# Squares of the out projection and twenty weight sums from VectorE to GpSimd, in a hybrid encoder layer

## The chip, the cores and the metric

The kernel runs on one core of a Trainium2 chip. The metric is device time in microseconds (us), the median of several runs. The core has five engines with instruction queues of their own: TensorE (PE, its weight loads listed as PEld), VectorE (DVE), ScalarE (ACT), GpSimd (POOL) and SyncE (SP, which here only issues DMAs). Each engine works through its queue in order, and semaphores make it wait for the others.

## The reference

One layer of an encoder, for 1024 tokens of width 1024, all in float32:

```
hn   = rmsnorm(x, norm_mix)
proj = hn @ w_in                      # split into two groups of heads
o_a  = window_gqa_sink(...)           # window of 128 to both sides, sink logit
o_b  = neighbourhood_attention(...)   # 2-D window with a learned bias
mix  = concat(rmsnorm(o_a, norm_a), rmsnorm(o_b, norm_b))
h    = x + mix @ w_out                # 1024 x 1024
hn   = rmsnorm(h, norm_ffn)
g    = hn @ w_gate; u = hn @ w_up     # 1024 x 2816 each
g    = conv3(g, conv_w) + conv_b      # along the tokens, per feature
h    = h + (silu(g) * u) @ w_down     # 2816 x 1024
out  = rmsnorm(h, norm_final)         # rmsnorm(x, g) = x * rsqrt(mean(x*x) + 1e-6) * g
```

The change touches the stretch from `mix @ w_out` over the sums of squares of `rmsnorm(h, norm_ffn)` to the first columns of `hn @ w_gate` and `hn @ w_up`.

## The kernel before

**Layout.** Activations stand transposed: 128 features on the partitions, tokens along the free axis. The 1024 features are eight tiles, numbered by d or k, and the 1024 tokens two halves (h) of 512. A "half tile" is 128 x 512. `at(k, h)` is half h of tile k of the residual stream h1. Products keep float32 accuracy by splitting each operand into a high and a low float16 part. A high part is made by ScalarE (a scaled copy), the low part by VectorE (the operand minus the high part: L1151 and L1068 for weights, L1096 for `w_out`, L1184 for activations). Three matmuls then stand for one: high by high, high by low, low by high.

**Out projection** (the loop before L1300). For each half h and each of the eight output tiles d, which I write (h, d), `product16` (L176) issues twelve matmuls (four tiles with three each) into one of three PSUM banks; the other four input tiles went into h1 earlier. `settle_out` (L1196) follows:

- L1199, VectorE: h1 = bank * scale + h1, with priority 300 in the scheduler.
- L1200: h1 goes to DRAM by a DMA of ScalarE's queue; it is read again only in the last stage.
- L1203, ScalarE: the square of the half tile.
- L1205, VectorE: for d = 1 to 3, the square plus the running total.

So the first four squares of a half are one addend, and d = 4 to 7 are four more. `sum_up` (L1210) gives each addend to PE as four matmuls of a single column against a tile of 1/1024 (L1216), accumulated in a narrow bank of 128 x 4: one number for each token. `inverse_root` (L1219) adds 1e-6 (L1221, VectorE) and raises to the power -1/2 (L1222, GpSimd). `widen` (L259) then spreads the four columns over all partitions with four PE transposes (L263). `normed` (L1225; L1227, VectorE) multiplies h1 by this and by the gain, for tiles K1 (0 to 3) or K2 (4 to 7). `operands` splits the result (ScalarE, L1184). An older helper, `inverse_power` (L217), does the same from one full total: four transposes (L221), a reduce over VectorE (L223), scaling and 1e-6 (L224) and the power on GpSimd (L225); the two attention groups use it earlier in the kernel.

For half 0 `inverse_root` stands at (1, 1), `widen`, `normed` of K1 and their operands at (1, 2), `normed` of K2 at (1, 4).

**FFN by seven products.** The input tiles K1 and K2, the gate and up columns, and the two token halves make a 2 x 2 block product, computed with seven block products in place of eight. With g1, g2 the K1 and K2 rows of the gate weights and u1, u2 those of the up weights, the weights' operands are "11" = g1, "12" = g2, s1 = u1 + u2, s2 = s1 - g1, s4 = g2 - s2, s3 = g1 - u1, "22" = u2. The sums are made in one tile `ws` of each unit (`head_weights`, L1233; L1237 for s1, `sub`, L1229, for the others) and then split. On the other side stand the normed halves and their differences t1 to t4 (`sub`, L1229, in place in h1). One output tile of gate and up together is a unit; product p1 uses "11", p2 "12", p5 s1 and t1, p6 s2 and t2, p3 s4, p7 s3 and t3, p4 "22" and t4. Each is twelve matmuls (`group`, L1174 to L1178).

The first four units go through the products side by side (L1463 to L1521): p1 and p2 of units 0 and 1, p1 of 2 and 3, p2 of 2 and 3, then p5, p6, p3, p7, p4 of all four. Half 1's norm is needed from p5 on. Its sum and `inverse_root` stand after p2 of unit 0, `widen` after p2 of unit 1. The weights' sums of these units are made early: s1 and s2 during the out projection, s4 at (1, 4) to (1, 7), s3 and "22" in the loops of p3 and p7.

**What sets the order.** PE's instructions keep the order of the program. The other engines' order comes from the scheduler, which takes what is ready, moved ahead by `high_priority(offset=...)`; `behind(name)` holds an instruction back until the marked one stands in the order. After the change the lines below L1205 carry smaller numbers; the names and the arithmetic stay.

Of the kernel before, what the change touches and what calls it, by code (L numbers as in the profile page):

```python
# [13 lines left out]
F32 = mybir.dt.float32  # L14
# [8 lines left out]
KT = D // 128  # L23
# [40 lines left out]
def hybrid_layer(tc, xT, w_in, w_out, w_gate, w_up, w_down, small, sink, rpb, consts, rope, out):  # L64
    nc = tc.nc
    with ExitStack() as ctx:
# [25 lines left out]
        def bank(name, tag):  # L92
            return psum.tile([128, HALF], F32, name=name, tag=tag)
# [123 lines left out]
        def inverse_power(sq, dim, tag):  # L217

            ps = bank("st", tag)
            for c in range(4):  # L220
                nc.tensor.transpose(ps[:, c * 128:(c + 1) * 128], sq[:, c * 128:(c + 1) * 128], ident)  # L221
            v = cpool.tile([128, 4], F32, name="v4", tag="v4", bufs=4)
            nc.vector.tensor_reduce(v, ps[:, :].rearrange("p (c w) -> p c w", w=128), axis=mybir.AxisListType.X, op=ALU.add)  # L223
            nc.vector.tensor_scalar(v, v, 1.0 / dim, EPS, op0=ALU.mult, op1=ALU.add)  # L224
            nc.gpsimd.tensor_tensor(v, v, minus_half, op=ALU.pow)  # L225
            return v
# [965 lines left out]
        B = {}  # L1192
        late, total, addends, narrow, ADDED = [], [None, None], [], [None, None], (4, 4)
        at = lambda k, h: h1[k][:, tsl(h)]

        def settle_out():  # L1196
# [5 lines left out]
            with tc.high_priority(offset=300):  # L1202
                nc.scalar.activation(s2, at(d, h), AF.Square)  # L1203
                if 0 < d < ADDED[h]:
                    nc.vector.tensor_tensor(s2, s2, total[h], op=ALU.add)  # L1205
            total[h] = s2
            if d >= ADDED[h] - 1:
                addends.append((h, d, s2))

        def sum_up(until=2 * KT):  # L1210
            while addends and KT * addends[0][0] + addends[0][1] <= until:
                h, d, s2 = addends.pop(0)
                if d == ADDED[h] - 1:
                    narrow[h] = bank("ss", "pt")
                for c in range(4):
                    nc.tensor.matmul(narrow[h][:, c:c + 1], s2[:, c * 128:(c + 1) * 128], ones[:, 0:1], start=c == 0 and d == ADDED[h] - 1,  # L1216
                                     stop=d == KT - 1, skip_group_check=True)

        def inverse_root(h):  # L1219
            v = cpool.tile([128, 4], F32, name="v4", tag="v4", bufs=4)  # L1220
            nc.vector.tensor_scalar(v, narrow[h][:, 0:4], EPS, None, op0=ALU.add)  # L1221
            nc.gpsimd.tensor_tensor(v, v, minus_half, op=ALU.pow)  # L1222
            return v

# [4 lines left out]
        sub = lambda o, x, y: nc.vector.tensor_tensor(o, x, y, op=ALU.subtract)  # L1229

        wsum = [fpool.tile([128, 4, 128], F32, name="ws", tag="tt", bufs=8) for _ in range(HEAD)]

        def head_weights(i, name):  # L1233
            f, t = FO[i], wsum[i]
            g, u = head_raw[f]
            if name == "s1":
                nc.vector.tensor_tensor(t, u[:, 0:4], u[:, 4:8], op=ALU.add)  # L1237
            elif name == "s2":
                sub(t, t, g[:, 0:4])
            elif name == "s4":  # L1240
                sub(t, g[:, 4:8], t)
            elif name == "s3":
                sub(t, g[:, 0:4], u[:, 0:4])
            else:
                t = u[:, 4:8]
# [8 lines left out]

        S1_AT, S2_AT, S4_AT, SETTLE_AT, PURE_AT = [(0,3),(0,3),(0,4),(0,5)], [(1,0),(1,1),(1,2),(1,3)], [(1,4),(1,5),(1,6),(1,7)], {(0,1):0,(0,3):2}, {(0,2):(0,1),(0,4):(2,3)}
        for d in range(WO_EARLY, KT):
# [4 lines left out]
        for h in range(2):  # L1261
            for d in range(KT):
                if h == 0 and len(wo) < KT:
                    wo.append(load_wo(len(wo), fpool))
                ps = bank("pj", ("o", "s", "pj")[(h * KT + d) % 3])
                for _ in product16(ps, wo[d], mg[4:8], h):
                    pass
                late.append((d, h, ps))
                sum_up(KT * h + d - 2)
                if h == 1 and d == 1:  # L1270
                    with tc.high_priority(offset=300):
                        v = inverse_root(0)
                settle_out()
# [4 lines left out]
                for when, name in ((S1_AT, "s1"), (S2_AT, "s2"), (S4_AT, "s4")):  # L1278
                    for i, x in enumerate(when):
                        if x == (h, d):  # L1280
                            head_weights(i, name)
                if h == 1 and d == 2:
                    wide = widen(v, "pt")
                    normed(0, wide, K1)
                    B[1, 1] = operands([at(k, 0) for k in K1], "mix", "mix")
                if h == 1 and d == 4:
                    normed(0, wide, K2)
                    B[2, 1] = operands([at(k, 0) for k in K2], "mix", "mix")
# [175 lines left out]
        units[0].p1()  # L1464
        units[1].p1()
        units[0].p2()
        with tc.high_priority(offset=300):
            sum_up()
            v = inverse_root(1)
        units[1].p2()  # L1470
# [417 lines left out]
```

## Time and profile before

| | before |
|---|---|
| runs, us | 1036.99, 1037.27, 1037.58 |
| median, us | 1037.27 |
| span of the profiled execution, us | 1035.9 |
| PE matmuls, busy us | 1011.7 (98%) |
| VectorE, busy us | 880.0 (85%) |
| ScalarE, busy us | 679.3 (66%) |
| GpSimd, busy us | 214.1 (21%) |
| DMA | 191.28 MB |

The span runs from the first to the last instruction of one profiled execution; for that execution no other time is recorded, so the 1.4 us between it and the median stand for what lies around the span. Busy times count the work of each engine without its waits. In a row of groups, `out<-in` names the tiles, then come the shapes and types, the count, the busy time with the mean in nanoseconds of one, and the idle time ahead with what ended it. A row of the timeline is the start in us, the length, the engine and the instruction, and in brackets a wait and its releaser; the length of a row of several instructions (x4) runs from the start of the first to the end of the last.

### The profile page before, as it was taken

Reading aid. Unit: us, or ns where it says so; the run is one execution under the profiler, and the core shown is the slowest. Engines: PE = TensorE matmul, PEld = TensorE weight load, DVE = VectorE, ACT = ScalarE, POOL = GpSimd, SP = SyncE. Lnnn points to the kernel's source line nnn. Section 1 sums busy time; section 2 is a strip of 40 time slices with the busy share of each in tenths; the row PEclk is TensorE's granted clock in tenths of the full one; section 3 lists DMA queues with packets and bytes.
Section 4 is the critical chain, followed back from the end, with each engine's and each line's share of the span. In section 5 each row is a group of like instructions: output and inputs, shape, how many; then the busy total and the mean of one; then the engine's idle time right before and its main releaser. Section 6 shows DMA issues by size and latency. Waiting matters only on the chain.

```text
span 1035.9 us, 15696 instructions
## 1 busy us (share of the span) xinstructions
PE 1011.7 (98%) x5102; PEld 577.3 (56%) x5102; DVE 880.0 (85%) x1748; ACT 679.3 (66%) x1243; POOL 214.1 (21%) x341
## 2 busy tenths in 40 slices
PE   9998999999999999999999999999999999999996
PEld 7776777777775545544444444444444444444446
DVE  6699998766898699899898988888888879899875
ACT  8567787767687587645777777754535656655551
POOL 2235455676866301000000000000000000000002
PEclk9999999999999999999999999999999999999998
DMA  9447473676689775300687867733232778878744
GB/s 347 155 98 149 109 139 83 151 168 140 134 180 224 213 276 193 121 1 21 222 266 261 276 241 250 251 111 133 82 112 102 240 252 297 301 250 264 255 153 163
DMA packets 144275, 191.28 MB, mean 185 GB/s; under 512 B 77376, under 2 KB 88640, under 8 KB 144192
## 3 DMA queue, kind: packets, MB, share of 16 engines
q1 hardware_dynamic: 133536, 164.51, 54.7%
q10 hardware_dynamic: 10656, 25.76, 6.4%
q8 instruction: 40, 0.66, 0.2%
q14 instruction: 43, 0.35, 0.1%
HBM read 132.81 MB, written 28.57 MB: 156 GB/s over the span
## 4 chain that ended last, share of the span: by engine, by line
PE 71%; DVE 6%; ACT 1%; DMA 1%; issue 1%; POOL 0%; ACTq 0%; DVEq 0%; SPq 0%; POOLq 0%
PE dn L1177 6%; PE dn L1178 6%; PE dn L1176 6%; PE pj L180 6%; PE z L1176 5%; PE z L1177 5%; PE z L1178 5%; PE y L1176 4%; PE y L1177 4%; PE y L1178 4%; PE x L1176 4%; PE x L1177 4%; PE x L1178 3%; PE pj L172 2%; PE pj L174 2%; PE pj L173 2%
## 5 line engine op out<-in xcount | busy, mean ns | idle before, releaser
L1178 PEld LDWEIGHTS <-wlo 128*128 128x128 f16 x898 | 87.9, 98 | 101.3 <-DVE wlo L1151 0.2
L1176 PEld LDWEIGHTS <-whi 128*128 128x128 f16 x898 | 88.1, 98 | 100.3
L1177 PEld LDWEIGHTS <-whi 128*128 128x128 f16 x898 | 87.9, 98 | 100.3 <-issue 0.2
L1178 PE MATMUL dn<-xd,wlo 128*128 128x512 f16 (+1 forms) x330 | 120.4, 365 | 0.0
L1177 PE MATMUL dn<-xd,whi 128*128 128x512 f16 (+1 forms) x330 | 120.4, 365 | 0.0
L1176 PE MATMUL dn<-xd,whi 128*128 128x512 f16 (+1 forms) x330 | 120.4, 365 | 0.0
L172 PE MATMUL pj<-xgh,whi 128*128 128x512 f32 x248 | 106.8, 431 | 0.8 <-ACT whi L156 0.8
L1177 PE MATMUL z<-hg,whi 128*128 128x512 f16 x264 | 100.1, 379 | 0.0
L1178 PE MATMUL z<-hg,wlo 128*128 128x512 f16 x264 | 100.1, 379 | 0.0
L1176 PE MATMUL z<-hg,whi 128*128 128x512 f16 x264 | 100.1, 379 | 0.0
L466 ACT ACTIVATE p<-p,nm 128x385 f32<-128x385 f32 (+3 forms) x128 | 74.8, 585 | 38.0 <-DVE nm L462 33.3
L174 PE MATMUL pj<-xgh,wlo 128*128 128x512 f32 x248 | 97.9, 395 | 1.4 <-POOL wlo L157 1.4
L173 PE MATMUL pj<-xgl,whi 128*128 128x512 f32 x248 | 97.5, 393 | 0.0
L1150 ACT ACTIVATE whi<-ws,m 128x512 f16<-128x512 f32 (+1 forms) x96 | 65.9, 709 | 35.6 <-DVE ws L1317 19.5
L1151 DVE SCALAR_TENSOR_TENSOR wlo<-ws,m,whi 128x512 f16<-128x512 f32 (+1 forms) x96 | 70.2, 741 | 17.8 <-ACT whi L1150 17.6
L1031 POOL TENSOR_TENSOR back<-back,cst 128x4 f32<-128x4 f32 (+1 forms) x7 | 2.8, 396 | 356.7 <-DVE back L1030 356.7
L1165 ACT ACTIVATE scan<-scan 128x1024 f32<-128x1024 f32 (+1 forms) x60 | 61.1, 1019 | 17.0 <-DMA scan<-in_w_down_dram 12.3
L1150 ACT ACTIVATE whi<-raw,m 128x512 f16<-128x512 f32 (+1 forms) x78 | 51.4, 700 | 17.9 <-DMA raw<-in_w_down_dram 12.7
L1151 DVE SCALAR_TENSOR_TENSOR wlo<-raw,m,whi 128x512 f16<-128x512 f32 (+1 forms) x78 | 55.4, 732 | 7.5 <-ACT whi L1150 6.9
L1176 PE MATMUL y<-hg,whi 128*128 128x512 f16 x160 | 60.6, 379 | 0.0
L1177 PE MATMUL y<-hg,whi 128*128 128x512 f16 x160 | 60.6, 379 | 0.0
L1178 PE MATMUL y<-hg,wlo 128*128 128x512 f16 x160 | 60.6, 379 | 0.0
(291 smaller groups left out, 2465.5 us busy)
## 6 DMA issues: line engine op xcount, KB each, us to landing
xd<-x SPq DMA_DIRECT2D x77, 256.0 KB, 5.4
raw<-in_w_down_dram SPq DMA_DIRECT2D x64, 256.0 KB, 3.8
x<-c ACTq DMA_DIRECT2D x22, 512.0 KB, 3.5
scan<-in_w_gate_dram SPq DMA_DIRECT2D x18, 512.0 KB, 4.7
scan<-in_w_up_dram SPq DMA_DIRECT2D x18, 512.0 KB, 4.3
raw<-in_w_gate_dram SPq DMA_DIRECT2D x18, 512.0 KB, 3.8
raw<-in_w_up_dram SPq DMA_DIRECT2D x18, 512.0 KB, 4.4
raw<-in_w_in_dram SPq DMA_DIRECT2D x32, 256.0 KB, 3.1
```

The source lines that it names most:

```text
L172: nc.tensor.matmul(ps, w[0], x[0][:, tsl(h)], start=first, stop=False)
L173: nc.tensor.matmul(ps, w[0], x[1][:, tsl(h)], start=False, stop=False)
L174: nc.tensor.matmul(ps, w[1], x[0][:, tsl(h)], start=False, stop=last)
L180: nc.tensor.matmul(ps, a, b, start=i == 0 and b is x[h][0] and a is w[0], stop=i == len(ws) - 1 and a is w[1])
L466: nc.scalar.activation(p[:, 0:e], p[:, 0:e], AF.Exp, bias=nm, scale=-1.0, accum_out=sm)
L1031: nc.gpsimd.tensor_tensor(back, back, unit_back.to_broadcast([128, n]), op=ALU.mult)
L1150: mark["whi"] = nc.scalar.activation(hi, src, AF.Copy, scale=by)
L1151: nc.vector.scalar_tensor_tensor(lo, src, by, hi, op0=ALU.mult, op1=ALU.subtract)
L1165: nc.scalar.activation(t, t, AF.Square, accum_out=dst)
L1176: nc.tensor.matmul(ps, w[0], x[0], start=first and i == 0, stop=False, skip_group_check=True)
L1177: nc.tensor.matmul(ps, w[0], x[1], start=False, stop=False, skip_group_check=True)
L1178: nc.tensor.matmul(ps, w[1], x[0], start=False, stop=last and i == len(ws) - 1, skip_group_check=True)
```

## The change

1. **Sums of squares.** `sum_up`, `inverse_root` and the narrow bank go. All eight squares of a half are added up into one total: d = 1 to 6 on GpSimd, d = 7 on VectorE. The total goes through `inverse_power` (four transposes, reduce, scaling, power): for half 0 behind the first three matmuls of (1, 3), for half 1 after p1 of unit 1 and before p2 of unit 0.
2. **Half 0's norm.** `widen` and `normed` of K1 move from (1, 2) to (1, 4), with priority 150; `normed` of K2 from (1, 4) to (1, 5).
3. **Twenty sums on GpSimd.** s1, s2, s4 and s3 of the first four units, and the four differences for t4. s2 is held behind half 0's sum of d = 6, the s4, s3 and the differences behind the last power (mark "power" in L225).
4. **s4 of the first units** moves, sum and split, from (1, 4) to (1, 7) into the loop of p2 of units 2 and 3.

The diff, cut to its core:

```diff
-            nc.gpsimd.tensor_tensor(v, v, minus_half, op=ALU.pow)
+            mark["power"] = nc.gpsimd.tensor_tensor(v, v, minus_half, op=ALU.pow)
...
                 nc.scalar.activation(s2, at(d, h), AF.Square)
-                if 0 < d < ADDED[h]:
-                    nc.vector.tensor_tensor(s2, s2, total[h], op=ALU.add)
+                if d:
+                    mark["sum", d, h] = (nc.vector if d == KT - 1 else nc.gpsimd).tensor_tensor(s2, s2, total[h], op=ALU.add)
             total[h] = s2
-            if d >= ADDED[h] - 1:
-                addends.append((h, d, s2))
...
+        def slow(o, x, y, after):
+            with behind(after):
+                nc.gpsimd.tensor_tensor(o, x, y, op=ALU.subtract)
...
             if name == "s1":
-                nc.vector.tensor_tensor(t, u[:, 0:4], u[:, 4:8], op=ALU.add)
+                nc.gpsimd.tensor_tensor(t, u[:, 0:4], u[:, 4:8], op=ALU.add)
             elif name == "s2":
-                sub(t, t, g[:, 0:4])
+                slow(t, t, g[:, 0:4], ("sum", KT - 2, 0))
             elif name == "s4":
-                sub(t, g[:, 4:8], t)
+                slow(t, g[:, 4:8], t, "power")
             elif name == "s3":
-                sub(t, g[:, 0:4], u[:, 0:4])
+                slow(t, g[:, 0:4], u[:, 0:4], "power")
...
-                for _ in product16(ps, wo[d], mg[4:8], h):
-                    pass
+                for i, _ in enumerate(product16(ps, wo[d], mg[4:8], h)):
+                    if (h, d, i) == (1, 3, 0):
+                        with tc.high_priority(offset=300):
+                            v = inverse_power(total[0], D, "pt")
                 late.append((d, h, ps))
-                sum_up(KT * h + d - 2)
-                if h == 1 and d == 1:
-                    with tc.high_priority(offset=300):
-                        v = inverse_root(0)
...
-                if h == 1 and d == 2:
+                if h == 1 and d == 4:
                     wide = widen(v, "pt")
-                    normed(0, wide, K1)
-                    B[1, 1] = operands([at(k, 0) for k in K1], "mix", "mix")
-                if h == 1 and d == 4:
+                    with tc.high_priority(offset=150):
+                        normed(0, wide, K1)
+                        B[1, 1] = operands([at(k, 0) for k in K1], "mix", "mix")
+                if h == 1 and d == 5:
                     normed(0, wide, K2)
...
         units[1].p1()
+        with tc.high_priority(offset=300):
+            v = inverse_power(total[1], D, "pt")
         units[0].p2()
-        with tc.high_priority(offset=300):
-            sum_up()
-            v = inverse_root(1)
         units[1].p2()
...
-        for u in units[2:]:
+        for i, u in enumerate(units[2:]):
             u.p2()
+            for k in (2 * i, 2 * i + 1):
+                head_weights(k, "s4")
...
         for k in K1:
             sub(at(k, 0), at(k, 1), at(k, 0))
-            sub(at(k, 1), at(k + 4, 0), at(k, 1))
+        for k in K1:
+            slow(at(k, 1), at(k + 4, 0), at(k, 1), "power")
```

How this stands in the queues, in two places. GpSimd, from the end of half 0's out projection to half 1's power. Before, these rows follow each other (`back` and `taps` are the convolution's taps, `v4` the narrow result of a half):

```order
L1031 TENSOR_TENSOR back_5079<-back_5079,cst_89 128x2
L1034 TENSOR_SCALAR taps_5082<-par_79,back_5079 128x3
L1034 TENSOR_SCALAR taps_5084<-par_79,back_5079 128x3
L1222 TENSOR_TENSOR v4_5236<-v4_5236,minus_half_87 128x4
L1222 TENSOR_TENSOR v4_5483<-v4_5483,minus_half_87 128x4
```

After the change the stretch from half 0's sum of d = 6 to the power of half 0 reads as follows (`s2` are squares and their totals, `ws` the tile of a unit's weight sums, `rw` its raw weights; L1205 adds squares, L1216 is `slow`, L225 the power):

```order
L1205 TENSOR_TENSOR s2_5163<-s2_5163,s2_5142 128x512
L1216 TENSOR_TENSOR ws_4954<-ws_4954,rw_4745 128x512
L1216 TENSOR_TENSOR ws_4955<-ws_4955,rw_4747 128x512
L1216 TENSOR_TENSOR ws_4956<-ws_4956,rw_4749 128x512
L1216 TENSOR_TENSOR ws_4957<-ws_4957,rw_4751 128x512
L1205 TENSOR_TENSOR s2_5221<-s2_5221,s2_5199 128x512
L1205 TENSOR_TENSOR s2_5244<-s2_5244,s2_5221 128x512
L225 TENSOR_TENSOR v4_5261<-v4_5261,minus_half_87 128x4
```

Between the taps and the power there was nothing; now the four s2 and two sums of half 1 stand ahead of half 0's power.

VectorE, around half 1's norm. Before (L1221 is the addition of 1e-6, L1151 a low part of s4, L1317 and L1330 sums for the unit behind the first four, L1227 `normed`, L1229 `sub`):

```order
L1221 TENSOR_SCALAR v4_5483<-ss_5363 128x4
L1151 SCALAR_TENSOR_TENSOR wlo_5374<-ws_4955,m_5006,whi_5373 128x512
L1317 TENSOR_TENSOR ws_6006<-raw_5973 128x512
L1151 SCALAR_TENSOR_TENSOR wlo_5400<-ws_4956,m_5074,whi_5399 128x512
L1151 SCALAR_TENSOR_TENSOR wlo_5426<-ws_4957,m_5074,whi_5425 128x512
L1330 TENSOR_TENSOR ws_6046<-raw_5971,raw_5973 128x512
L1227 SCALAR_TENSOR_TENSOR h1_4134<-h1_4134,cst_89,sw_5500 128x512
```

After (L223 and L224 are the reduce and its scaling; L1303 and L1316 are the lines that were L1317 and L1330, L1210 the one that was L1227, `normed`):

```order
L1303 TENSOR_TENSOR ws_5984<-raw_5951 128x512
L223 TENSOR_REDUCE v4_5426<-st_5421 128x4
L1316 TENSOR_TENSOR ws_6024<-raw_5949,raw_5951 128x512
L224 TENSOR_SCALAR v4_5426<-v4_5426 128x4
L1151 SCALAR_TENSOR_TENSOR wlo_5527<-ws_4954,m_5006,whi_5526 128x512
L1151 SCALAR_TENSOR_TENSOR wlo_5532<-ws_4955,m_5006,whi_5531 128x512
L1151 SCALAR_TENSOR_TENSOR wlo_5551<-ws_4956,m_5074,whi_5550 128x512
L1151 SCALAR_TENSOR_TENSOR wlo_5556<-ws_4957,m_5074,whi_5555 128x512
L1210 SCALAR_TENSOR_TENSOR h1_4134<-h1_4134,cst_89,sw_5458 128x512
```

All four s4 splits now stand between the reduce and the first norm, and each takes its `ws` from GpSimd, which makes it after the power.

More of the change, by code (lines that the diff above doesn't have):

```diff
@@ L1192, in hybrid_layer @@
         B = {}
-        late, total, addends, narrow, ADDED = [], [None, None], [], [None, None], (4, 4)
+        late, total = [], [None, None]
         at = lambda k, h: h1[k][:, tsl(h)]
@@ L1203, in settle_out @@
                 nc.scalar.activation(s2, at(d, h), AF.Square)
-                if 0 < d < ADDED[h]:
-                    nc.vector.tensor_tensor(s2, s2, total[h], op=ALU.add)
+                if d:
+                    mark["sum", d, h] = (nc.vector if d == KT - 1 else nc.gpsimd).tensor_tensor(s2, s2, total[h], op=ALU.add)
             total[h] = s2
-            if d >= ADDED[h] - 1:
-                addends.append((h, d, s2))
[L1210 to L1223, printed above, removed]
         def normed(h, wide, ds):
@@ L1253, in hybrid_layer @@
         s1_places = []
-        S1_AT, S2_AT, S4_AT, SETTLE_AT, PURE_AT = [(0,3),(0,3),(0,4),(0,5)], [(1,0),(1,1),(1,2),(1,3)], [(1,4),(1,5),(1,6),(1,7)], {(0,1):0,(0,3):2}, {(0,2):(0,1),(0,4):(2,3)}
+        S1_AT, S2_AT, S4_AT, SETTLE_AT, PURE_AT = [(0,3),(0,3),(0,4),(0,5)], [(1,0),(1,1),(1,2),(1,3)], [None] * HEAD, {(0,1):0,(0,3):2}, {(0,2):(0,1),(0,4):(2,3)}
         for d in range(WO_EARLY, KT):
```

## The prediction

> **What bounds the kernel now.** The page first: TensorE (PE) is busy 98% of the span.
>
> ```profile
> span 1035.9 us, 15696 instructions
> PE 1011.7 (98%) x5102; PEld 577.3 (56%) x5102; DVE 880.0 (85%) x1748; ACT 679.3 (66%) x1243; POOL 214.1 (21%) x341
> ```
>
> Then the table of 10 us stretches over the place of the change (the out projection runs from 369 to 419, the first four FFN units from 419 to 494): busy time of PE, weight loads, VectorE (DVE), ScalarE, GpSimd (POOL), then clock and DMA.
>
> ```profile
> core 0: us, PE busy (x) PEld busy (x) DVE busy (x) ACT busy (x) POOL busy (x), PEclk, DMA share, GB/s
> 385.00:395.00 10.00, 10.00 (x61) 6.11 (x59) 10.00 (x17) 8.58 (x15) 1.68 (x3) 1.00 0.64 211
> 395.00:405.00 10.00, 10.00 (x59) 5.87 (x57) 8.72 (x15) 5.91 (x10) 1.39 (x1) 1.00 0.35 124
> 475.00:485.00 10.00, 10.00 (x48) 4.51 (x46) 10.00 (x12) 4.73 (x5) 0.00 (x0) 1.00 0.01 2
> ```
>
> PE never waits here, VectorE is full without making it wait, and GpSimd is nearly idle. So only two things count: PE work taken out, and new waits of PE. VectorE time saved is worth nothing by itself.
>
> **The change part by part.** *PE work.* From PE's timeline (start, length, what):
>
> ```profile
> 357.91 1.04 PE L221 MATMUL st<-cst,sq 128*128 128x128 f32 x8
> 358.78 0.59 PE L180 MATMUL pj<-mg,whi 128*128 128x512 f16 x2
> ...
> 386.19 0.95 PE L1216 MATMUL ss<-ones,s 128*128 128x1 f32 x8
> 387.00 2.75 PE L180 MATMUL pj<-mg,wo 128*128 128x512 f16 x12
> ...
> 403.18 0.60 PE L263 MATMUL sw<-cst,v 128*128 128x128 f32 x4
> 403.62 7.93 PE L180 MATMUL pj<-mg,wo 128*128 128x512 f16 x36
> ...
> 426.75 1.84 PE L1216 MATMUL ss<-ones,s 128*128 128x1 f32 x16
> 428.46 0.38 PE L1176 MATMUL x<-hg,wp 128*128 128x512 f16 x1
> ```
>
> A narrow sum holds PE 0.81 (386.19 to 387.00). Eight stand alone and two together (1.71): 8 x 0.81 + 1.71 = 8.2 us go. Two groups of four transposes come; eight take 0.87. Net gain on PE: 7.3 us, all of it kept if PE still never waits. One matmul takes 0.216 ((2.75 - 0.38)/11), a product of 12 takes 2.59, four widening transposes 0.44.
>
> *VectorE.* Starts in a row give what an instruction costs the queue: 0.66 for a SCALAR_TENSOR_TENSOR, 0.61 for a half-tile TENSOR_TENSOR ((2.53 - 0.69)/3), 0.33 for the small reduce, 0.07 for the smallest.
>
> ```profile
> 376.57 0.74 DVE L1199 SCALAR_TENSOR_TENSOR h<-pj,wo_back,h 128x512 f32<-128x512 f32 x1
> 377.23 0.41 DVE L1011 TENSOR_REDUCE m<-wm 128x2 f32<-128x256 f32 x1
> 377.56 0.74 DVE L1096 SCALAR_TENSOR_TENSOR wo<-wr,wo_by,wo 128x512 f16<-128x512 f32 x1
> 378.23 0.16 DVE L243 TENSOR_SCALAR m<-m 128x2 int32<-128x2 int32 x1
> ...
> 421.69 2.53 DVE L1184 TENSOR_TENSOR hg<-h,hg 128x512 f16<-128x512 f32 x4
> ```
>
> Six sums of squares and twenty sums (26) leave; two last addends and two transposed reduces come: 22 x 0.61 = 13.4 us off VectorE. PE did not wait for them, so they are worth nothing unless VectorE is late.
>
> *GpSimd, and what it does to VectorE.* It gets 32 half-tile operations with two SBUF inputs. Its nearest row is the weight split L157, 1.29 us: 32 x 1.29 = 41 us of work. The row that decides is what happens when both engines run such operations:
>
> ```profile
> 210.17 1.29 POOL L157 TENSOR_TENSOR wlo<-raw,whi 128x512 fp32r<-128x512 f32 x1
> ...
> 289.27 1.74 POOL L157 TENSOR_TENSOR wlo<-raw,whi 128x512 fp32r<-128x512 f32 x1
> ```
> ```profile
> 287.78 0.74 DVE L863 SCALAR_TENSOR_TENSOR mixa<-mixa,gains,rstda 128x512 f32<-128x512 f32 x1
> ...
> 288.92 0.94 DVE L863 SCALAR_TENSOR_TENSOR mixa<-mixa,gains,rstda 128x512 f32<-128x512 f32 x1
> ...
> 290.20 1.36 DVE L863 SCALAR_TENSOR_TENSOR mixa<-mixa,gains,rstda 128x512 f32<-128x512 f32 x1
> ```
>
> GpSimd's 1.74 is 0.45 too long: it began working at 289.72, just as VectorE's operation ended (289.86). VectorE's next, issued at 290.20, is 0.62 too long: it began at 290.82, 1.10 after GpSimd. The two take turns, and one turn of GpSimd holds VectorE 1.09; in a full VectorE queue, where the next operation would have started 0.06 later anyway, it costs 1.03. An operation that reads PSUM is not stretched: in the stage where GpSimd is busiest L273, with one input in PSUM, keeps 0.68 on average, L863 goes from 0.74 to 0.94.
>
> ```profile
> L273 DVE TENSOR_TENSOR t<-pj,rstd 128x512 f32<-128x512 f32 x24 | 16.4, 682 | 1.7 <-PE pj L174 1.6
> L863 DVE SCALAR_TENSOR_TENSOR mixa<-mixa,gains,rstda 128x512 f32<-128x512 f32 x8 | 7.5, 937 | 0.0
> ```
>
> In a full queue GpSimd mostly gets in, not always:
>
> ```profile
> 294.77 2.02 DVE L328 SCALAR_TENSOR_TENSOR kb<-t,cst,ka 128x512 fp32r<-128x512 f32 x2
> 388.91 1.27 DVE L1237 TENSOR_TENSOR ws<-rw 128x512 f32<-128x512 f32 x2
> ```
> ```profile
> 295.45 0.80 POOL L486 TENSOR_SCALAR y<-p,sm 128x256 f32<-128x256 f32 x1
> 389.08 1.16 POOL L1031 TENSOR_TENSOR back<-back,cst 128x2 f32<-128x2 f32 x1 [7.12 <-DVE back L1030]
> ```
>
> Two L328 take 1.41 alone, here 2.02: GpSimd got between. L1031 (0.20 alone) waited out both L1237. I take 0.85 us per GpSimd operation that meets a full queue; its bounds are 0 (never in the way) and 1.03.
>
> The Trainium skill's page "SBUF — State Buffer", section "Who interferes with whom", calls this an exclusive lock: a VectorE instruction with two SBUF inputs and a GpSimd instruction that reads SBUF block each other for the whole instruction. It speaks against this change, and the trace agrees in kind, but the hold measured is 1.09 of 1.29; by the page's whole instruction ten turns would cost 2 us more (an estimate).
>
> *First wait: the transposes.* The order places four transposes of half 0's total behind three matmuls of half 1's product 3. Without waits PE is there at 386.19 + 5 x 2.59 + 3 x 0.216 = 399.8. VectorE makes the last addend itself. From L1199 at 376.57 its queue has 7 L1199 and 16 weight splits (L1096, L1068) at 0.66, 2 reduces at 0.33, 8 smallest at 0.07, and the addend, 0.69: 17.1, so 393.7. GpSimd has 12 operations before that point (six sums, four s1, two s2); two fall beside L1199, which reads PSUM, ten meet splits: 10 x 0.85 = 8.5. The total is ready at 402.2: PE waits 2.4. At 1.03 it would be 4.2, at 0 none (6 us spare).
>
> *Second wait: the power.* After the addend VectorE has three L1199, four L1151, the reduce (the row's 0.69, 0.61 in the queue) and 0.16: 5.4, and one turn, 0.85. Then GpSimd's queue has a sum (1.29) ahead of the power (1.39): ready at 402.2 + 5.4 + 0.85 + 2.7 = 411.15. PE comes to the widening at 402.2 + 0.44 + 9 x 0.216 + 2.59 = 407.2: it waits 4.0.
>
> ```profile
> L223 DVE TENSOR_REDUCE v<-st 128x4 f32<-128x512 f32 x6 | 4.0, 688 | 6.6 <-PE st L221 6.5
> ```
> ```profile
> 401.01 1.39 POOL L1222 TENSOR_TENSOR v<-v,minus_half 128x4 f32<-128x4 f32 x1 [10.16 <-DVE v L1221]
> ```
> ```profile
> 401.56 0.72 ACT L1150 ACTIVATE whi<-ws,m 128x512 f16<-128x512 f32 x1
> ```
>
> *Third wait: units' t1.* The four s4 splits (L1151) now stand on VectorE ahead of half 1's norm, and each waits for GpSimd. Widened at 411.6, VectorE does 11 x 0.66 + 10 x 0.61 = 13.4 and one turn (425.8), reduces and a w sum 1.4 (427.2), power 1.4, first s4 1.3, its high part 0.7 (430.6), four splits each with a turn, 4 x 1.51 (436.6), four norms 2.64, one turn, four differences 2.44, first low part 0.69: 443.3. PE is there at 411.6 + 3 x 2.59 + 2 x 2.59 + 0.44 + 2 x 2.59 + 0.44 + 4 x 2.59 = 441.0, and needs it 0.2 later: it waits 2.1, and 0.5 more at k = 2 behind a norm.
>
> *Fourth wait: t2.* VectorE has 15 TENSOR_TENSOR and four norms, 11.9, up to the end of the last t2 low part, with three GpSimd differences (2.55) in between: 443.2 + 14.45 = 457.65. PE needs it at 441.0 + 2.6 + 10.36 + 2.16 = 456.1: 1.5.
>
> Behind it lies t4:
>
> ```profile
> 448.60 1.89 DVE L1184 TENSOR_TENSOR hg<-h,hg 128x512 f16<-128x512 f32 x3
> ...
> 477.83 0.69 DVE L1184 TENSOR_TENSOR hg<-h,hg 128x512 f16<-128x512 f32 x1
> ```
> ```profile
> 483.28 0.38 PE L1176 MATMUL z<-hg,whi 128*128 128x512 f16 x1
> ```
>
> Before, the last t2 part (the first of the three) begins at 448.60, the last t4 part ends at 478.5, and is read from 483.28 on: 4.8 spare. Now VectorE is 8.4 later at t2 (457.0), does eight operations less after it (4.9), and PE comes 3.2 later: some 4 us stay, so no wait.
>
> At nothing: ScalarE's squares and splits are the same; the spills to DRAM follow L1199, and nobody reads them before the last stage; the taps (L1034), now behind sums in GpSimd's queue, are read only by the convolutions after the units' fifth product. If these covers went, the worst is one GpSimd operation, 1.3 us.
>
> The sum: 2.4 + 4.0 + 2.6 + 1.5 = 10.5 of waits less 7.3: **+3.2 us**. Against the profiled span that is 1039.1; the runs' median, 1037.27, lies 1.4 above that span, so 1040.5.
>
> **The rivals.** *The turns cost little.* Moving the turn by 0.05 us moves the sum by about 1 us (0.80: +2.1; 0.90: +4.2). Below 0.60 the kernel is faster, from 0.60 to 0.80 within 0.2% (2.1 us, about what a measurement can tell from no change). If GpSimd loses most turns, as L1031 did, and fits beside PSUM readers, all waits go: 1037.3 - 7.3 = 1030.0. For it: one of the two rows above, and 13.4 us off VectorE. Against: L863 and L328, stretched each time. This is faster, where I forecast slower.
>
> *The turns are halved.* Waits and gain cancel: 1035.2 to 1039.3.
>
> *PE comes back cold.* The first matmuls of the kernel run at half speed and the clock falls when PE stops:
>
> ```profile
> 0.98 4.64 PE L134 MATMUL warm_ps<-ones 128*128 128x128 f32 x20 [0.98 <-POOL eps L104]
> ```
> ```profile
> 1030.00:1036.00 6.00, 0.00 (x0) 0.00 (x0) 1.54 (x4) 0.00 (x0) 1.25 (x2) 0.51 0.54 176
> ```
> ```profile
> PE o L596 <- DMA turned<-stage: 1.8, 1, 1.8
> ```
>
> 0.23 us each against 0.11 for L221. No wait above 1.8 us shows inside the kernel, so whether 2 to 4 us slow the clock is open. If both first waits do, each returns at half speed for up to 4.6 us, so loses 2.3: 1040.5 + 4.6 = 1045.1. The Trainium skill's page "TensorE: Matmul & The Clock Gate", Part 1, puts the idle window at about 3.4 us; by it only the second wait would count.
>
> **How the numbers follow.** My forecast, with turns between 0.80 and 1.03 (1039.3 to 1043): 0.42. Cold PE on top: 0.08. Cancelled: 0.20. Small turns, faster: 0.30, since the walk has some sixty steps and its sign hangs on a third of one price. Faster 0.30, same 0.20, slower 0.50. The range leaves out the lowest (waits all gone) and the highest: 1031 to 1045.
>
> **What would show it.** In the changed profile: no L1216 matmuls, and eight L221 transposes between 395 and 425; PE waiting for the addend at L221 some 2 us and for the power at L263 some 4 us; L1068 and L1151 on VectorE above 1 us on average instead of 0.75; GpSimd's sums at 1.3 to 2 us. Wrong if L1068 stays at 0.75 while GpSimd adds, if PE's first wait comes elsewhere, or if PE is busy 10 in 10 from 385 on.

## The result, and the profile after

| | before | after |
|---|---|---|
| runs, us | 1036.99, 1037.27, 1037.58, 1038.43 | 1046.18, 1046.87, 1046.91, 1048.92 |
| median, us | 1037.42 | 1046.89 |
| ratio (95% interval) | | 1.0086 (1.0074 to 1.0098) |

The change makes the kernel some 9 us slower, where 3.2 were forecast. The first two lines of the page of the profile after:

```profile
span 1044.8 us, 15586 instructions
PE 1009.9 (97%) x5030; PEld 571.2 (55%) x5030; DVE 886.2 (85%) x1726; ACT 676.8 (65%) x1243; POOL 262.5 (25%) x373
```

VectorE has 22 instructions less and is busy 6.2 us more (880.0 before); the experiments below show that this is the turns. The 10 us stretches, columns as before, two from before the change and then three from after it:

```profile
405.00:415.00 10.00, 10.00 (x54) 5.23 (x52) 9.29 (x16) 7.86 (x14) 0.00 (x0) 1.00 0.68 219
435.00:445.00 10.00, 10.00 (x48) 4.54 (x47) 10.00 (x18) 7.89 (x14) 0.00 (x0) 1.00 0.00 0
```

```profile
core 0: us, PE busy (x) PEld busy (x) DVE busy (x) ACT busy (x) POOL busy (x), PEclk, DMA share, GB/s
395.00:405.00 10.00, 6.42 (x30) 2.72 (x28) 10.00 (x11) 5.57 (x9) 7.32 (x6) 1.00 0.21 77
405.00:415.00 10.00, 8.15 (x25) 3.49 (x25) 9.10 (x12) 6.55 (x11) 7.64 (x6) 0.66 0.34 106
435.00:445.00 10.00, 5.55 (x28) 2.49 (x26) 7.88 (x8) 7.03 (x12) 10.00 (x8) 1.00 0.20 59
```

PE, 10.00 in each of them before, has two holes, and its clock falls in one. In the list of PE's waits from 360 to 520 us (sum, times, longest):

```profile
PE st L221 <- DVE s L1205: 5.1, 2, 4.9
PE x L1176 <- ACT gs L1345: 4.4, 2, 2.8
PE sw L263 <- POOL v L225: 0.8, 1, 0.8
PE x L1176 <- ACT c L1339: 0.6, 1, 0.6
```

PE's timeline (start, length, what, and in brackets the wait):

```profile
391.76 9.66 PE L180 MATMUL pj<-mg,wo 128*128 128x512 f16 x44
406.31 1.09 PE L221 MATMUL st<-cst,s 128*128 128x128 f32 x4 [4.88 <-DVE s L1205]
407.19 7.27 PE L180 MATMUL pj<-mg,wo 128*128 128x512 f16 x21
415.30 0.65 PE L263 MATMUL sw<-cst,v 128*128 128x128 f32 x4 [0.84 <-POOL v L225]
```

A row ends 0.16 later than the next one could begin (0.38 less 0.216), so each wait delays PE by 0.16 more than its bracket. From the rows: 5.05 at the transposes; 3.0 by the slow clock behind them (21 matmuls in 7.27 where 4.70 is usual, and 0.88 for 0.44 at the transposes); 1.0 for the power; 0.36 at half 1's transposes; 2.93, 1.83 and 0.77 at the units' banks; 0.33 for a low part of `w_out`. That makes 15.3, less 7.3 of PE work: +8.0. The spans differ by 8.9, of which 0.9 was there before the change's place (the same matmul of the out projection starts at 370.44 and at 371.32).

What VectorE and GpSimd did ahead of the first two waits:

```profile
384.64 1.27 DVE L243 TENSOR_SCALAR m<-m 128x2 int32<-128x2 int32 x1
385.82 1.86 DVE L1096 SCALAR_TENSOR_TENSOR wo<-raw,wo_by,wo 128x512 f16<-128x512 f32 x1
...
404.41 1.75 DVE L1205 TENSOR_TENSOR s<-s,s 128x512 f32<-128x512 f32 x1
...
412.10 0.68 DVE L223 TENSOR_REDUCE v<-st 128x4 f32<-128x512 f32 x1
```
```profile
412.99 1.28 POOL L1205 TENSOR_TENSOR s<-s,s 128x512 f32<-128x512 f32 x1 [0.34 <-ACT s L1203]
414.21 1.03 POOL L225 TENSOR_TENSOR v<-v,minus_half 128x4 f32<-128x4 f32 x1
```

L1096 takes 0.74 alone, the addend 0.68, the integer operation on two columns 0.16: each lost one turn of GpSimd, 1.07 to 1.12. Twelve instructions of VectorE are stretched from 379 to 406, ten of them by 0.93 to 1.14 each and two by less; together that is 11.2 us. The power then stood behind the reduce, which began 4.9 after the transposes' end, and behind a sum.

ScalarE at the second hole, with GpSimd's s4 sums beside it:

```profile
435.64 0.72 ACT L1150 ACTIVATE whi<-ws,m 128x512 f16<-128x512 f32 x1 [3.72 <-POOL ws L1216]
...
437.50 0.58 ACT L1345 ACTIVATE gs<-x 128x512 f32<-128x512 f32 x1
...
440.25 0.72 ACT L1150 ACTIVATE whi<-ws,m 128x512 f16<-128x512 f32 x1 [0.98 <-POOL ws L1216]
...
441.92 0.57 ACT L1345 ACTIVATE gs<-x 128x512 f32<-128x512 f32 x1
```
```profile
434.32 5.90 POOL L1216 TENSOR_TENSOR ws<-rw,ws 128x512 f32<-128x512 f32 x4
```

PE had ended unit 0's p2 product at 432 and unit 1's at 435; their banks' copies (`gs`, L1345) stood in ScalarE's queue behind s4 high parts that waited for GpSimd, and p1 of units 2 and 3 needs those banks. This place is not in the forecast.

### The profile page after: what moved, and what is told of

Its sections match the earlier page's. It is cut to its first block, busy times and chain, and to the rows that moved or that the text cites. A ratio compares the mean times of both kernels' runs of the same rounds, so it can differ in the third digit from the quotient of the medians.

```text
span 1044.8 us, 15586 instructions
## 1 busy us (share of the span) xinstructions
PE 1009.9 (97%) x5030; PEld 571.2 (55%) x5030; DVE 886.2 (85%) x1726; ACT 676.8 (65%) x1243; POOL 262.5 (25%) x373
## 4 chain that ended last, share of the span: by engine, by line
PE 57%; DVE 14%; DMA 4%; issue 2%; ACT 2%; POOL 1%; SPq 0%; ACTq 0%; DVEq 0%; POOLq 0%
PE z L1178 5%; PE z L1176 5%; PE z L1177 5%; PE dn L1178 4%; PE dn L1177 4%; PE dn L1176 4%; PE y L1178 4%; PE y L1176 4%; PE y L1177 4%; PE x L1176 3%; PE x L1178 3%; PE x L1177 3%; PE pj L180 2%; PE pj L172 2%; PE pj L174 2%
## 5 line engine op out<-in xcount | busy, mean ns | idle before, releaser
L1151 DVE SCALAR_TENSOR_TENSOR wlo<-ws,m,whi 128x512 f16<-128x512 f32 (+1 forms) x96 | 74.0, 780 | 21.4 <-ACT whi L1150 21.2
L1569 DVE SCALAR_TENSOR_TENSOR xd<-xd,m 128x512 f16<-128x512 f32 x77 | 55.2, 749 | 6.4 <-ACT xd L1568 6.4
```

The costliest lines, as they stand in the source:

```text
L1151: nc.vector.scalar_tensor_tensor(lo, src, by, hi, op0=ALU.mult, op1=ALU.subtract)
L1569: nc.vector.scalar_tensor_tensor(lo, t[:, HALF:S], by, hi, op0=ALU.mult, op1=ALU.subtract)
```

## The experiments

Each run is compared with the kernel before on the same chip (medians there 1037.6 to 1038.75), so the ratio is what to compare; the expectations are in us on the 1037.3 of the kernel before.

**The parts of the change.** First the change with all additions on VectorE: the edits below, cut to the words that change; the same for squares alone (e2) and for the twenty sums alone (e3).

```diff
-  (nc.vector if d == KT - 1 else nc.gpsimd).tensor_tensor(s2, s2, total[h], op=ALU.add)
+  nc.vector.tensor_tensor(s2, s2, total[h], op=ALU.add)
-  nc.gpsimd.tensor_tensor(t, u[:, 0:4], u[:, 4:8], op=ALU.add)      # s1
+  nc.vector.tensor_tensor(t, u[:, 0:4], u[:, 4:8], op=ALU.add)
-  nc.gpsimd.tensor_tensor(o, x, y, op=ALU.subtract)                  # slow: s2, s4, s3, t4
+  nc.vector.tensor_tensor(o, x, y, op=ALU.subtract)
```

> The change with all its new GpSimd work (the twelve sums of squares and the twenty sums) on VectorE; the transposes and the moved places stay. Turns theory (VectorE and GpSimd hold each other up, about 1.03 us a turn): no VectorE split above 0.8 us; half 0's total is ready before PE comes to the transposes (wait under 0.5), the power some 1.7 us late, and VectorE, with 5 us more work than before and PE 7.3 us earlier, makes PE wait some 4 us in the units: 1034 to 1039. Rival (the new places and the single addend themselves cost the time, whichever engine adds): still 1043 or more.

Measured: 1039.3, ratio 1.0013 (1.0004 to 1.0023). The page's first lines:

```profile
span 1037.5 us, 15560 instructions
PE 1007.8 (97%) x5030; PEld 569.9 (55%) x5030; DVE 884.7 (85%) x1758; ACT 678.2 (65%) x1243; POOL 218.4 (21%) x341
```

So the new places alone, without GpSimd, eat the 7.3 us and 1.4 more (PE waits 1.25 at the transposes and 3.9 for the first units' operands, and loses 1.7 to the slow clock behind these), and GpSimd's part is the other 7.6. The rival's 1043 did not come, but its effect, 8.7 us, is about half of the 16.3 that the change loses in all. VectorE: 32 instructions more than with the change, at 0.61 each 19.5 us, yet 1.5 us less busy time. The 32 on GpSimd had therefore lengthened VectorE's others by 21.0, **0.66 each: more than the 0.61 that one costs VectorE itself**.

> The change with the sums of squares alone back on VectorE; the twenty sums stay on GpSimd. Turns theory: four s1 and two or three s2 still meet VectorE's queue ahead of the total (6 turns), so PE waits some 2 us at the transposes and some 5 us at the power, and the 5.5 us behind ScalarE's bank copies stay, since the s4 sums stay on GpSimd: about 1043. Rival (GpSimd's serial chain of six sums is what makes the total late): the first two waits are gone, 1040 or less.

Measured: 1046.0, ratio 1.0073 (1.0058 to 1.0088), 3 us above the expected 1043. The total was in time, but the low part of `w_out` was 2.5 late, the power 4.5 and the copies 4.1 in all; and the slow clock behind the power, which I had not counted, took 3.0 (the widening in 0.91 for 0.44, 36 matmuls in 10.46 where 7.93 is usual). The serial chain of sums on GpSimd was not the cause.

> The change with the twenty sums back on VectorE; the sums of squares stay on GpSimd. Turns theory: six turns ahead of the total, so PE waits up to 1 us at the transposes, some 6 us for the power (VectorE's reduce is late and a sum stands ahead of the power), nothing behind ScalarE's copies, 1.5 in the units: about 1038.5. Rival (the serial chain of sums on GpSimd is the delay): the first two waits stay at 9 us, 1041 or more.

Measured: 1040.7, ratio 1.0030 (1.0016 to 1.0044): 0.3 at the transposes, 4.7 for the power, 1.5 by the slow clock behind it, 0.7 at the copies. The time lies between the two expectations; the first two waits are 5.0 and not 9. The twenty sums cost more than the squares.

Then one group of the twenty at a time on GpSimd, all else on VectorE (where, s4 apart, it is no longer held behind a mark): s1 and s2, s4, and the rest.

> The change with only s1 and s2 (eight sums) on GpSimd, all else of its GpSimd work on VectorE; to be read against the run with all on VectorE (1039.3) and the one with all twenty sums on GpSimd (1046.0). Place theory: the cost lies ahead of half 0's norm, where these eight meet VectorE's full queue (a turn of 1.03 for a saving of 0.61 each, 3.4 us), hold up the w_out split and stand ahead of the power; with the slow clock after the stall up to 3 more: 1043 to 1046. Rival (each of the twenty costs the same, 0.34 us): 1042.

Measured: 1043.0, ratio 1.0036 (1.0021 to 1.0051): 2.5 for `w_out`, 4.5 for the power, 1.8 by the slow clock behind it. The 1043.0 is on a chip where the kernel before takes 1038.75. By the ratios, s1 and s2 cost 2.4 us more than all on VectorE; that is the rival's figure (2.7), not the 3.7 or more of the place theory, so this run does not tell the two apart. The trace, moreover, is of the fastest of ten executions (1039.4); what the others lost besides is not shown.

> The change with only s4's four sums on GpSimd. Place theory: ScalarE's copies of the units' second products stand behind s4 high parts that wait for GpSimd, behind half 1's power: 2 to 4 us, 1041 to 1043. Rival (each of the twenty costs 0.34): 1040.7.

Measured: 1042.8, ratio 1.0041 (1.0024 to 1.0057). ScalarE's timeline, and the PE wait that follows:

```profile
426.02 0.72 ACT L1150 ACTIVATE whi<-ws,m 128x512 f16<-128x512 f32 x1 [2.42 <-POOL ws L1216]
427.72 0.72 ACT L1150 ACTIVATE whi<-ws,m 128x512 f16<-128x512 f32 x1 [0.98 <-POOL ws L1216]
428.35 1.13 ACT L1183 ACTIVATE hg<-h 128x512 f16<-128x512 f32 x2
```
```profile
PE x L1177 <- DVE hg L1184: 4.5, 5, 3.1
```

The size is as expected (by the ratios 2.9 us more than e1, where the rival has 1.4), the place only in part: s4 high parts wait for GpSimd at the head of ScalarE's queue, but what stands behind them here is two operands of the second products, not the copies, and two operands ahead of these are stretched by turns on VectorE (3.13 us for two L1184 that take 1.28). With s4 on VectorE (e1) the same wait was 2.5 in all. This execution is one of the slowest of ten (1045.7); 3.3 us of its time were lost in the down projection, far from the change.

> The change with only s3 and the differences for t4 (eight operations) on GpSimd. Place theory: VectorE has some 4 us to spare there, nobody waits: 1039 to 1040. Rival (each of the twenty costs 0.34): 1042.

Measured: 1039.6, ratio 1.0009 (0.9998 to 1.0020): nothing beside e1, where the rival has 2.7 us. An equal price for each of the twenty thus falls by e10 and e11: the cost of the twenty lies in twelve of them. Against e1's 1.0013, s1 and s2 add 0.0023, s4 0.0028, the tail -0.0004 and the squares (e3) 0.0017: with the new order's 0.0013 that makes 1.0077 of the 1.0086 (each of these shares is known to some 0.002).

**The turns by themselves.** The kernel before, with work on GpSimd that nobody waits for, behind each L1199 of d = 1 to 6:

```diff
                 nc.scalar.activation(s2, at(d, h), AF.Square)
+                if 0 < d < KT - 1:
+                    idle = fpool.tile([128, S], F32, name="junk", tag="junk", bufs=1)
+                    nc.gpsimd.tensor_tensor(idle[:, 0:HALF], at(d, h), at(d, h), op=ALU.add)        # e7
+                    nc.gpsimd.tensor_tensor(idle[:, 0:4], at(d, h)[:, 0:4], minus_half, op=ALU.pow)  # e8
```

> The kernel before with twelve half-tile additions on GpSimd that nobody waits for, one behind each L1199 of d = 1 to 6 of both halves, into a scratch tile: the same places and size as the change's sums of squares, and no work taken from any engine. Turns theory: VectorE loses up to 1.03 us to each (less those beside its PSUM readers), about 5 us by half 0's power and 10 us by the units, with some 0.8 and 4.8 us to spare there: 1043 to 1047. Rival (GpSimd's work beside VectorE costs only queue places): at most 0.5 us from the add ahead of half 0's power, 1037 to 1038.

> The same kernel with a power of 128x4 in place of each of the twelve additions: GpSimd is busy about as long (1.0 to 1.4 us each) at the same places, but reads little. Turns theory by bytes read: VectorE keeps its lengths, 1037 to 1038.5. Rival (any GpSimd instruction of this length holds VectorE for its whole time): as with the additions, 1043 to 1047.

Measured: 1042.2, ratio 1.0037 (1.0024 to 1.0050), with the additions, and 1039.1, ratio 1.0008 (0.9999 to 1.0018), with the powers. The engines' lines and two instructions on VectorE of the one,

```profile
PE 1013.7 (97%) x5102; PEld 578.5 (56%) x5102; DVE 886.3 (85%) x1748; ACT 678.2 (65%) x1243; POOL 229.6 (22%) x353
```
```profile
392.16 2.05 DVE L1240 TENSOR_TENSOR ws<-rw 128x512 f32<-128x512 f32 x2
```

and of the other:

```profile
PE 1012.8 (98%) x5102; PEld 577.8 (56%) x5102; DVE 880.2 (85%) x1748; ACT 678.8 (65%) x1243; POOL 226.9 (22%) x353
```
```profile
390.16 1.28 DVE L1240 TENSOR_TENSOR ws<-rw 128x512 f32<-128x512 f32 x2
```

Twelve additions (1.04 us alone, up to 1.43 here) lengthen VectorE by 6.3 us, twelve powers of about the same length by 0.2. So the turn goes by what GpSimd moves, 128x512 against 128x4, and not by how long it is busy (reading, writing and the kind of operation were not varied apart), and the time comes from it. The additions' time is 0.8 below the range expected, by the ratio 1.9, since PE waited only 1.3 and 1.5 us; the powers' time is 0.6 above its range, by the ratio within it.

**s4's place.** Back on VectorE, at (1, 4) to (1, 7) (e4), or still on GpSimd but behind the copies (e6):

```diff
-  S4_AT ... [None] * HEAD                    # e4
+  S4_AT ... [(1,4),(1,5),(1,6),(1,7)]
...
-  slow(t, g[:, 4:8], t, "power")
+  sub(t, g[:, 4:8], t)
...
             u.p2()                           # e4 and e6
-            for k in (2 * i, 2 * i + 1):
-                head_weights(k, "s4")
```
```diff
         for i, u in enumerate(units):        # e6
             u.p5()
+            with behind("unit"):
+                head_weights(i, "s4")
```

> The change with s4 of the first units put back to VectorE and to its old places in the out projection; all else stays. Theory: the 5.5 us that PE waits for ScalarE's copies of the units' banks come from the s4 high parts that stand ahead of them in ScalarE's queue and wait for GpSimd; they go, the first two waits (9 us) stay: about 1040. Rival (they only cover that t1 is late on VectorE): PE then waits at the fifth products instead, 1043 or more.

Measured: 1049.9, ratio 1.0115 (1.0092 to 1.0138): slower still. The waits at the banks fell from 5.5 to about 3, but the s4 parts now stood ahead of the reduce on VectorE:

```profile
PE st L221 <- DVE s L1205: 4.9, 1, 4.9
PE sw L263 <- POOL v L225: 4.5, 1, 4.5
```

I had taken the first two waits as fixed at 9 us; they hang on what stands ahead of the reduce, and the slow clock came behind both (36 matmuls in 10.43 where 7.93 is usual, behind the second). The run therefore does not tell what s4 off GpSimd is worth at the copies.

> The changed kernel with s4 of the first units (sums on GpSimd, both parts of the split) behind ScalarE's last copy of the units' second products, in the loop of the fifth products. If the s4 high parts that wait for GpSimd ahead of those copies cost PE its 5.5 us there, these waits go and half 1's t1 comes some 6 us earlier on VectorE, so that PE doesn't wait there either: 1041 to 1042. If t1 and t2 were the true limit behind them: 1045 or more.

Measured: 1046.8, ratio 1.0079 (1.0062 to 1.0095): no gain. The waits at the copies are gone, as expected, and PE comes to the fifth products 4.3 us earlier than in the change (from the same matmul of the out projection, at 371.32 there and at 372.26 here). The first row is the change's, the second e6's:

```profile
451.08 0.38 PE L1176 MATMUL y<-hg,wp 128*128 128x512 f16 x1
447.76 0.38 PE L1176 MATMUL y<-hg,wp 128*128 128x512 f16 x1
```

Of these 4.3 us 3.4 are lost again behind them, 2.2 of it to an addition into a unit's bank. Ahead of them, the slow clock took 1.4 less behind the first wait, PE waited 1.3 longer for the power (which came at the same moment), and the clock was slow once more behind that, for 1.7. The rival's number is right, though PE does not wait for t1 or t2: most of what left one place came back at others.

**The slow clock.** 22 matmuls more on PE ahead of half 0's transposes:

```diff
             ps = bank("st", tag)
+            for _ in range(keep_busy):       # 22 for half 0
+                nc.tensor.matmul(ps, wo[3][0][0], mg[4][0][0], start=True, stop=True)
```

> The changed kernel with 22 more matmuls of 128x512 on PE (4.75 us by 0.216 each, their result is overwritten) ahead of half 0's four transposes, so that PE works through its wait for the addend. If the half-speed clock after that wait costs what it seems to (21 matmuls in 7.27 us instead of 4.70, and 0.44 at the transposes: 3.0 us), the clock stays at 1.00 and the time falls by 3 us, to 1044. If VectorE and GpSimd bring half 0's power at the same moment whatever PE's clock is (about 415 us into the span), PE only waits longer for it: 1046 to 1047.

Measured: 1054.6, ratio 1.0151 (1.0134 to 1.0169). PE's timeline up to the widening:

```profile
401.96 4.91 PE L221 MATMUL st<-mg,wo 128*128 128x512 f16 x22
406.92 0.66 PE L223 MATMUL st<-cst,s 128*128 128x128 f32 x4
407.42 4.70 PE L180 MATMUL pj<-mg,wo 128*128 128x512 f16 x21
415.98 0.65 PE L265 MATMUL sw<-cst,v 128*128 128x128 f32 x4 [3.87 <-POOL v L227]
```

The clock stays up (4.70 again), and the widening comes at 415.98 all the same, 0.7 after the change's 415.30 in an execution that was 0.7 behind from the start. So the slow clock's 3.0 us lay beside the wait for the power. The time is no answer beyond that point, and neither expectation came: behind the wait of 3.87 the clock fell after all (the next 36 matmuls took 9.62, 1.7 more than usual), and the scheduler, given a longer PE, put two more scans of weight rows, which wait for their DMA, ahead of the first operands on ScalarE. The 8 us more than the change's time arise behind the widening.

**s2 behind the power.**

```diff
-  S2_AT ... [(1,0),(1,1),(1,2),(1,3)], slow(t, t, g[:, 0:4], ("sum", KT - 2, 0))
+  S2_AT ... [(1,3),(1,3),(1,4),(1,5)], slow(t, t, g[:, 0:4], "power")
```

> The changed kernel with s2 of the first units (sum on GpSimd, both parts of the split) behind half 0's power instead of behind half 0's sum of d = 6; all else stays. If the s2 parts ahead of reduce and power are the second wait: the addend is 1.4 us earlier (two turns less), the power is there before PE comes to the widening, so waits of 1.4 and 4 us go, the 5.5 us at ScalarE's copies stay: 1041 to 1043. If VectorE's backlog is only moved: 1045 or more.

Measured: 1049.4, ratio 1.0109 (1.0092 to 1.0126). The reduce comes at 407.43 in place of 412.10, and yet PE waits 3.5 for the power. ScalarE, GpSimd and VectorE there:

```profile
410.21 1.06 ACT L1165 ACTIVATE scan<-scan 128x1024 f32<-128x1024 f32 x1 [1.73 <-DMA scan<-in_w_gate_dram]
...
411.27 0.61 ACT L1203 ACTIVATE s<-h 128x512 f32<-128x512 f32 x1
```
```profile
412.02 1.26 POOL L1205 TENSOR_TENSOR s<-s,s 128x512 f32<-128x512 f32 x1 [2.19 <-ACT s L1203]
413.24 1.02 POOL L225 TENSOR_TENSOR v<-v,minus_half 128x4 f32<-128x4 f32 x1
```
```profile
407.43 0.68 DVE L223 TENSOR_REDUCE v<-st 128x4 f32<-128x512 f32 x1
...
416.29 0.98 DVE L1151 SCALAR_TENSOR_TENSOR wlo<-ws,m,whi 128x512 f16<-128x512 f32 x1 [7.24 <-ACT whi L1150]
```

The power stands behind a sum, that behind a square, that on ScalarE behind a scan that waits for its DMA; VectorE then stands idle for 7.24 us behind an s2 part that waits for GpSimd. The wait at the transposes fell from 4.9 to 3.7, as expected. For the rest neither of my two readings was it: VectorE's backlog is gone here, and the time is lost in queues that wait for each other, with 1.7 us of slow clock behind the power and 3.4 still at the copies.

**A faster version.** From e1, s2 of the first units behind (1, 7), still on VectorE (e12); then s3 and the differences for t4 on GpSimd as well, and s2 without its hold (e14).

```diff
-  S2_AT ... [(1,0),(1,1),(1,2),(1,3)]
+  S2_AT ... [(1,7),(1,7),(1,7),(1,7)]
-  slow(t, t, g[:, 0:4], ("sum", KT - 2, 0))
+  slow(t, t, g[:, 0:4], ("sum", KT - 2, 1))     # e12; e14: sub(t, t, g[:, 0:4])
```

> The change with all its GpSimd work on VectorE and s2 of the first units moved from (1, 0) to (1, 3) to behind (1, 7): an attempt at the faster kernel. If VectorE's full queue ahead of half 0's norm is what eats the 7.3 us of PE work saved, 5 us less of it there makes the waits at the transposes and at the first units' operands (5 us with all on VectorE) go, and some 2 to 3 us come back at t1: 1034 to 1037. If VectorE's total work up to t4 is the limit (5 us more than before, PE 7.3 us earlier), they come back whole: 1038 to 1040.

Measured: 1037.2, ratio 0.9984 (0.9972 to 0.9995). Faster than before by 1.6 us. The waits for the first units' operands are gone, 1.3 at the transposes stayed, and others moved to the sixth and seventh products, among them

```profile
PE z L1178 <- DVE wlo L1151: 1.1, 1, 1.1
PE z L1177 <- DVE hg L1184: 0.7, 1, 0.7
```

> The faster version so far (all on VectorE, s2 behind (1, 7); 1037.2) with s3 and the differences for t4 on GpSimd. In that version PE waits some 3 us for VectorE at the sixth and seventh products. If a half-tile operation that goes to GpSimd costs VectorE about what it saves (0.66 against 0.61): 1036.7 to 1037.7, no difference. If it relieves VectorE, up to 3 us: 1034 to 1036.

Measured: 1036.3, ratio 0.9982 (0.9970 to 0.9993). These two waits are not in its profile, but by the intervals the two versions can't be told apart, and from the out projection's start to the first matmul of the down projection both traces take 450.6 and 450.5 us, where the kernel before takes 452.5. So the tail on GpSimd brings nothing here. Both beat the kernels before and after, but 5.3 of the 7.3 us of PE work are still lost (3.8 in the waits of e14's trace between 360 and 520 us).

## Why the prediction was wrong

The sign was right, and two thirds of the loss were not foreseen: 1040.5 with 1031 to 1045, measured 1046.9. Step by step, in us:

| term | forecast | measured |
|---|---|---|
| PE work | -7.3 | -7.3 (8.2 of narrow sums gone; transposes 0.44 at full clock) |
| transposes wait for the addend | 2.4 | 5.05 |
| widening waits for the power | 4.0 | 4.0: 1.0 of wait, 3.0 of slow clock |
| t1, then t2 | 2.6 and 1.5 | none |
| ScalarE's copies of the units' banks | 0 ("At nothing: ScalarE's squares and splits are the same") | 5.5 |
| smaller waits | 0 | 0.7 |
| sum | +3.2 | +8.0 |

The miss is 4.8 us: 2.7 at the transposes, 1.4 where waits at the copies came in place of those for t1 and t2, 0.7 in small waits. (The median was missed by 6.4: 0.9 more lay ahead of the change's place, 0.7 between span and median.)

**The step that failed** is the sentence quoted in the table. ScalarE's instructions are the same, but four of them had got a new, late supplier. I walked that lateness down VectorE's queue (to t1) and not down ScalarE's, where the copies that free PE's banks stood behind the same four. That cost 5.5 us at a place where I had put nothing. e6 shows it at the place itself: with the four behind the copies, the copies' wait goes and PE is 4.3 us earlier at the fifth products. (e10, with s4 alone on GpSimd, shows the same four holding up ScalarE's queue and costs 0.0028 more than e1, but what PE waits for there is operands, not copies.) With PE 5.5 us later, t1 was in time (its first low part ended at 449.06, PE came at 451.08), so the third and the fourth wait did not appear: one late chain, met at another place. Without the copies PE would have come at 445.6 and waited 3.5 for t1 (an estimate from these rows), so the walk down VectorE was right in kind, and leaving out ScalarE's made the sum too small by only some 2 us.

**The size that was off**, and the larger part of the miss, is the turn at the first wait: "I take 0.85 us per GpSimd operation that meets a full queue", ten of them, 8.5. Measured are 11.2, in twelve stretched instructions at 0.93 on average, and among these were three integer operations on two columns, counted as "0.07 for the smallest". 2.4 and the 2.7 missing make the 5.1 that came. The range allowed for 1.03, not for these. The Trainium skill's page "SBUF — State Buffer", section "Who interferes with whom", lists `tensor_scalar` among the operations that can take the shared pair, when their operands meet the conditions of a two-port mode; L243 at 1.27 for 0.16 agrees, and I had used the page for instructions with two inputs only.

**The rivals.** *Small turns* and *halved turns* fell: ahead of the total the turns were larger than forecast, and the waits grew to 15.3. (e7's twelve additions cost VectorE 6.3 us, 0.53 each with those that met no full queue.) *Cold PE* came, after the first wait alone, and cost nothing there (e5): the forecast's 4.6 on top was not to be added, since the power's time does not hang on PE. Where the slow clock comes behind the power, as in e2 and e4, nothing hides it, and it costs 3.0.

**What held:** the 7.3 us, and the power's lateness (e5, with the clock up, has the 4.0 as one wait: 3.87 and 0.16). Of the signs, the stretched splits came (L1068 1.13 us on average, L1151 from `ws` 0.97) and GpSimd's sums at 1.3 to 2 us. The "13.4 us off VectorE" did not come: its busy time rose by 6.2. That could have been seen in the forecast's own rows, as a turn of 0.85 is already more than the 0.61 that the operation costs on VectorE.

## What to carry to other kernels

Where VectorE's queue is full, an operation with its inputs in SBUF moved to GpSimd brings nothing if it costs VectorE a turn as long as itself (here 0.66 us against 0.61); ask for that price before counting the saving, and move only what falls where VectorE has time (here the tail, which cost nothing, and brought nothing either). When an operation gets a later supplier, walk down the queue of every engine that consumes it, not only the busiest one: a high part that waits at the head of ScalarE's queue held bank copies that PE needed. And PE work taken out is worth only what the other engines can follow: the same 7.3 us ended as +9 us in the change, +1.4 with the additions on VectorE, and -1.6 with four of them and their splits placed later (e12).

## What the runs showed of the hardware

- GpSimd's powers on 128x4 take 1.0 to 1.5 us and lengthen nothing on VectorE (880.2 against 880.0 us busy for twelve); additions on 128x512 of 1.04 us do (886.3).
- PE's clock after a wait: behind 4.88 us 21 matmuls took 7.27 in the changed kernel and 5.90 in e6, where 4.70 is usual; behind 3.67 us (e13) 4.70, no loss; behind 2.77 us none. Yet behind 2.93 us in e13 seven matmuls ran at half speed, in e1 eight behind 1.37 and 2.34 us with one matmul between them, and behind 2.19 us in e6, 9 us after the long wait, 36 took 9.62 where 7.93 is usual. The length of the wait alone does not tell. The Trainium skill's page "TensorE: Matmul & The Clock Gate", Part 1, puts the idle window at about 3.4 us and lets it run freely, so that the same wait may or may not fill it; 3.67 without a loss agrees with the second half of that, the losses behind shorter waits do not agree with the first.
- Executions of some kernels with such waits scatter more (ten each: e3 1038.5 to 1045.9, e9 1039.4 to 1046.1, e10 1038.8 to 1047.6; the kernel before, beside e9 and e10, 1036.9 to 1041.3 in 31). Why is not shown.
